# Turned groups' transfers to and from scratch issued by GpSimd in place of SyncE

## The chip, the cores and the metric

The kernel runs on one core of one Trainium2 chip. The metric is device time in microseconds: the median of 3 runs before the change is 1476.31 us (1476.15 to 1476.97).

## What is computed

The reference is one layer of a decoder trunk on 256 tokens of width 2048, in float32: a mixer (a state-space part with 32 heads and a gated short convolution), attention to 256 memory tokens, and a SwiGLU feed-forward part of width 5632. Each is added to the residual, with an RMS norm ahead of it, and a final norm follows. Cut to what matters:

```python
h = x
h = h + hybrid_mixer(rmsnorm(h, norm_mix), w_in, ..., w_out)     # 2048 -> 11296 -> 4096 -> 2048
h = h + memory_cross_attention(rmsnorm(h, norm_xa), rmsnorm(mem, mem_norm), w_q, w_k, w_v, w_o)
h = h + (silu(n @ w_gate) * (n @ w_up)) @ w_down                 # n = rmsnorm(h, norm_ffn)
return rmsnorm(h, norm_final)
```

Nearly all the work is products of 256 tokens with weights that are read once each.

## The kernel before

**Weights.** They come as a stream of 537 pieces, mostly 128 x 1024 (512 KB), in the order of a plan. SyncE loads each into one of 6 raw buffers, tile r (`load_to`, L214). ScalarE rounds it to a float32r high part, tile h (L254), and VectorE subtracts that from the piece to get the low part, tile l (L255); both have 4 buffers. TensorE then multiplies high by high, low by high and high by low: 12 matmuls of 512 columns for a piece, L328, L329 and L332. Some pieces are joined in pairs, where 7 products of blocks take the place of 8 (L657, L658, L660). For these, VectorE and ScalarE first form sums of the two pieces (`pair_sums`, L229 to L237), and corrections after it.

**Order.** The order of TensorE and SyncE is that of the code, since the kernel fixes it for those two engines. The instructions of ScalarE, VectorE and GpSimd are placed by a scheduler. The main loop runs in units of one or two pieces. `unit` loads some pieces ahead, calls the matmuls, and advances each of a list of generators by one step, so that work that follows a group of columns is spread over the next units.

**Turned groups.** A group of 512 columns is ready in PSUM with tokens on the partitions, and what follows needs features on the partitions. So VectorE transposes its 32 x 32 blocks (`turn_blocks`, L347, into tile b). `put` (L362) writes them to a scratch tile w in HBM with one DMA (L365), and `get` (L368) reads them back with one DMA (L372) in an order that moves the blocks to their places, 8 x 128 runs of 512 bytes, into tile f. There are 42 such groups:

- in the mixer, `group_post` (22 groups): what reads tile f there is L740, L848, L872 or L889
- after the output projection and after the attention, `to_features` (7 groups): L994 and L995
- in the attention, `heads` for keys and queries (2 groups): L1146 and L1148
- in the feed-forward part, `u_post` (11 groups): L1319 on ScalarE, then L1320 on VectorE

In the code there is one step of the generators, and so a unit, between the put, the get and the use; in `heads`, and in three calls of `to_features`, other numbers of steps. Both DMAs are issued by SyncE, in the place in its order where the generator calls them. Each waits there for what it needs: the put for VectorE's transposes, the get for the put's landing.

**GpSimd** has little to do: the masks of the decays (L714, L718), 24 in four runs of 6, each mask behind a load of decays that ScalarE's queue issues, and the small powers of the norms (L308, L903, L1400).

**The end of a group's work.** The norm's factor (L308) goes back to TensorE, which broadcasts it by transposes (`bcast`, L315), two units after it was asked for. The memory for DMAs that GpSimd issues is set when the program is built (`dynamic_dma_scratch_size=1024`, L1626); the change leaves that as it is.

Of the kernel before, what the change touches and what calls it, by code (L numbers as in the profile page):

```python
# [150 lines left out]
def trunk(tc, wst, vecs, xp, xtp, mp, mtp, wdt_in, nfin, outp):  # L151
    nc = tc.nc
# [8 lines left out]
    with ExitStack() as ctx:  # L161
# [18 lines left out]
        def nm(s):  # L180
            cnt[0] += 1
            return f"{s}{cnt[0]}"

        def slot(shape=(128, 512), dt=F32):
            return sp.tile(list(shape), dt, tag="s", name=nm("s"))
# [157 lines left out]
        def turn_blocks(src):  # L343

            t = bp.tile([128, 1024], F32, tag="b", name=nm("b"))
            for tb in range(2):
                nc.vector.transpose(t[:, tb * 512:tb * 512 + 512], src[tb])  # L347
            return t

        def scaled(accs, r, adds=None):  # L350

            o = [slot() for _ in range(2)]
            for tb in range(2):
                src = accs[tb]
                if adds is not None:
                    c, op = adds[tb]
                    tt(o[tb], src, c, op)
                    src = o[tb]
                act(o[tb], src, AF.Identity, scale=r[:, tb:tb + 1])  # L359
            return o  # L360

        def put(t):  # L362

            w = drp.tile([2, 128, 512], F32, tag="w", name=nm("w"), bufs=2)
            nc.sync.dma_start(w.rearrange("t p k -> p t k"), t.rearrange("p (t k) -> p t k", t=2))  # L365
            return w

        def get(w):  # L368


            d = fp.tile([128, 1024], F32, tag="f", name=nm("f"))
            nc.sync.dma_start(d.rearrange("p (x c) -> p x c", x=8),  # L372
                              w.rearrange("t (a i) (b c) -> (i b) (t a) c", a=4, b=4))
            return d.rearrange("p (x f j) -> p f x j", x=8, f=4)


# [218 lines left out]
        def group_post(n, accs):  # L595
            t = turn_blocks(scaled(accs, scales["x"], in_corr.pop(n, None)))
            yield
            w = put(t)
            yield
            d = get(w)  # L600
            yield
            if isinstance(groups[n], tuple):
                yield from posts[groups[n][0]](groups[n][1], d)
                return
            for f, (kind, _, j) in enumerate(groups[n]):
                p = posts[kind](j, d[:, f])
                if next(p, 0) is None:
                    procs.append(p)
                if f < 3 and not (kind == "xs" and j % 2 == 0):
                    yield  # L610
# [75 lines left out]
        for kt in range(KT):  # L686
            first_unit(kt)
            if kt == 10:
                c = 0
# [258 lines left out]
        for parts in in_units():  # L948
# [10 lines left out]
            _, n, c = keys[-1]  # L959
# [38 lines left out]
        def wait(k):  # L998
            for _ in range(k):
                yield  # L1000

        def to_features(n, gain, dst, steps=(1, 1, 1)):

            if steps is None:
                for i in range(2):
                    ps = msc()
                    for f in (2 * i, 2 * i + 1):
                        for tb in range(2):  # L1010
                            nc.tensor.transpose(ps[:, (f % 2) * T + tb * 128:(f % 2) * T + tb * 128 + 128],
                                                res[tb][n][:, f * 128:f * 128 + 128], ident)
                    for f in (2 * i, 2 * i + 1):
                        dst[4 * n + f] = gained(ps[:, (f % 2) * T:(f % 2) * T + T], gain, 4 * n + f)
                return
            t = turn_blocks([res[tb][n] for tb in range(2)])
            yield from wait(steps[0])
            w = put(t)
            yield from wait(steps[1])
            d = get(w)  # L1020
            yield from wait(steps[2])
            for f in range(4):
                dst[4 * n + f] = gained(d[:, f], gain, 4 * n + f)
# [86 lines left out]
        for i, parts in enumerate(units_o):  # L1110
            for j in (i, i + 1, i + 2):
                if j < len(units_o) and len(units_o[j][0]) == 2 and units_o[j][0][0] not in seven_a:
                    c = units_o[j][0][0][2]
# [6 lines left out]
            _, n, c = keys[0]  # L1120
# [12 lines left out]
        def heads(accs, r, dst, steps=(1, 1, 1)):  # L1133

            t = turn_blocks(scaled(accs, r))
            yield from wait(steps[0])
            w = put(t)
            yield from wait(steps[1])
            d = get(w)
            yield from wait(steps[2])  # L1140
            with tc.high_priority():
                for i in range(2):
                    a = slot()
                    o = a.rearrange("p (f x j) -> p f x j", f=2, x=8)
                    if i:
                        nc.vector.tensor_copy(o, d[:, 2:4])  # L1146
                    else:
                        nc.scalar.copy(o, d[:, 0:2])  # L1148
                    dst.append(a)

        KTs, Vs, qs = [], [], []
        for m, tiles in (("k", mh), ("q", h1g)):
            accs = [acc(), acc()]
            last = KT // 2 - 2
            for c in range(0, last, 2):
                unit([([(m, k)], lambda k=k: tok_mm(accs, (m, k), side_blocks(tiles, 2 * k), (0, 1), k == 0, False))
                      for k in (c, c + 1)])

            def last_mm(tb):
                for k in (last, last + 1):  # L1160
                    tok_mm(accs, (m, k), side_blocks(tiles, 2 * k), (tb,), False, k == last + 1)

            keys = [(m, last), (m, last + 1)]
            unit([(keys, lambda: last_mm(0)), (keys, lambda: last_mm(1))],
                 heads(accs, scales["mem"], KTs) if m == "k" else heads(accs, xa["sc"], qs, (2, 1, 0)))
# [96 lines left out]
        with tc.high_priority():  # L1262
            for mb in range(2):
                Vs.append(slot())
                c = scales["mem"][:, mb:mb + 1]
# [71 lines left out]
        for i, parts in enumerate(ffn_units()):  # L1337
# [6 lines left out]
            for part in parts:  # L1344
                m, n, c = part[0]
# [134 lines left out]
        for i, parts in enumerate(units):  # L1480
# [7 lines left out]
            if len(parts[0]) == 2:  # L1488
                _, n, c = keys[0]
# [141 lines left out]
```

## Time and profile before

| | |
|---|---|
| median of 3 runs | 1476.31 us |
| the profiled execution | 1478.79 us |
| its span | 1477.1 us |
| granted TensorE clock | 0.999 |
| busy: TensorE, VectorE, ScalarE, GpSimd | 99%, 87%, 60%, 3% |
| bytes from HBM and to it | 323.4 MB, 26.3 MB |

The span is the time from the first to the last instruction of one profiled execution. In the profile PE is TensorE, DVE VectorE, ACT ScalarE, POOL GpSimd and SP SyncE; SPq is SyncE's queue. A tile is named without its buffer's number. TensorE's matmuls overlap, so that a row of 390 ns stands for one every 227 ns. A wait is put down to what came last by the profile, and a wait of an engine that isn't the bound costs nothing by itself.

### The profile page before, as it was taken

The numbers are of one execution on the slowest core, as the hardware profiler recorded it, in microseconds if no ns is written. First come the engines' busy times: TensorE is split into PE (matmuls) and PEld (weight loads), VectorE is DVE, ScalarE is ACT, GpSimd is POOL, SyncE is SP. The second block draws the span as 40 slices with busy tenths as digits, with TensorE's granted clock in tenths as the row PEclk, the third lists the DMA queues.
The fourth block names the chain that finished last, engine by engine and source line by source line (L and its number), as shares of the span: only waits on it lengthen the run. The fifth ranks groups of instructions, "written<-read, shape, count | busy, mean of one in ns | idle before, by whom it ended". The sixth has DMA issues, their size and how long they took to land.

```text
span 1477.1 us, 18980 instructions
## 1 busy us (share of the span) xinstructions
PE 1461.6 (99%) x6568; PEld 1203.6 (81%) x6568; DVE 1279.7 (87%) x1865; ACT 885.4 (60%) x1263; POOL 38.5 (3%) x46
## 2 busy tenths in 40 slices
PE   9999999999999999999999999999999999999997
PEld 7778888888887888888888888888888887888886
DVE  6678899989999775897578999999999998979995
ACT  7576665967765544665466665556655554655663
POOL 0012000101000000000000000000000000000000
PEclk9999999999999999999999999999999999999999
DMA  9777758769677575777648766656676667765553
GB/s 362 248 251 263 259 202 296 253 215 313 224 258 261 193 262 188 253 270 279 224 171 295 265 220 224 220 215 225 228 247 247 220 228 229 268 228 190 195 201 112
DMA packets 151520, 350.91 MB, mean 238 GB/s; under 512 B 11616, under 2 KB 63232, under 8 KB 151424
## 3 DMA queue, kind: packets, MB, share of 16 engines
q1 hardware_dynamic: 142368, 342.83, 66.1%
q10 hardware_dynamic: 9056, 6.87, 1.6%
q8 instruction: 51, 0.84, 0.2%
q14 instruction: 45, 0.37, 0.1%
HBM read 323.40 MB, written 26.26 MB: 237 GB/s over the span
## 4 chain that ended last, share of the span: by engine, by line
PE 67%; DVE 1%; issue 0%; ACT 0%; DVEq 0%; POOLq 0%; POOL 0%
PE a L328 17%; PE a L329 17%; PE a L332 17%; PE m L660 3%; PE m L657 3%; PE m L658 3%; PE a L658 2%; PE a L657 2%; PE a L660 2%; PE m L1207 0%; PE m L1176 0%; PE m L804 0%; PE m L1195 0%; DVE g L1309 0%; DVE f L1292 0%
## 5 line engine op out<-in xcount | busy, mean ns | idle before, releaser
L254 ACT CAST h<-r 128x1024 fp32r<-128x1024 f32 (+1 forms) x539 | 562.3, 1047 | 401.7 <-PE a L329 190.0
L255 DVE TENSOR_TENSOR l<-r,h 128x1024 fp32r<-128x1024 f32 (+1 forms) x539 | 649.5, 1216 | 120.3 <-ACT h L254 114.9
L328 PE MATMUL a<-h,s 128*128 128x512 f32 x1671 | 655.0, 392 | 1.1 <-ACT h L254 1.1
L329 PE MATMUL a<-h,s 128*128 128x512 f32 x1671 | 651.0, 390 | 0.0
L332 PE MATMUL a<-l,s 128*128 128x512 f32 x1671 | 450.0, 390 | 0.0
L328 PEld LDWEIGHTS a<-h,s 128*128 128x128 f32 x1671 | 313.9, 188 | 68.2 <-ACT h L254 2.2
L332 PEld LDWEIGHTS a<-l,s 128*128 128x128 f32 x1671 | 313.7, 188 | 65.6 <-DVE l L255 0.4
L329 PEld LDWEIGHTS a<-h,s 128*128 128x128 f32 x1671 | 314.1, 188 | 64.0
L236 ACT CAST s<-b 128x512 fp32r<-128x512 f32 x110 | 67.6, 618 | 71.3 <-DVE b L229 65.4
L237 DVE TENSOR_TENSOR s<-b,s 128x512 fp32r<-128x512 f32 x110 | 75.6, 687 | 0.8 <-ACT s L236 0.7
L347 DVE STREAM_TRANSPOSE b<-s 128x512 f32<-128x512 f32 x62 | 40.9, 691 | 7.2 <-ACT s L359 7.2
L229 DVE TENSOR_TENSOR b<-r,r 128x512 f32<-128x512 f32 x55 | 37.7, 686 | 10.3 <-DMA r<-in_w_dram 9.8
L230 DVE TENSOR_TENSOR r<-r 128x512 f32<-128x512 f32 x55 | 37.9, 689 | 0.8
L232 DVE TENSOR_TENSOR r<-b,r 128x512 f32<-128x512 f32 x55 | 37.7, 686 | 0.1
L237 DVE TENSOR_TENSOR s<-r,s 128x512 fp32r<-128x512 f32 x55 | 37.7, 685 | 0.0
L236 ACT CAST s<-r 128x512 fp32r<-128x512 f32 x55 | 33.9, 617 | 6.2 <-DVE r L232 5.1
L231 DVE TENSOR_TENSOR b<-b,r 128x512 f32<-128x512 f32 x55 | 37.7, 685 | 0.0
L745 DVE SCALAR_TENSOR_TENSOR t<-t,vec,t 128x255 f32<-128x255 f32 (+2 forms) x72 | 32.4, 479 | 2.8 <-ACT t L742 2.3
L657 PE MATMUL m<-s,t 128*128 128x512 f32 x76 | 29.6, 389 | 0.0
L660 PE MATMUL m<-s,t 128*128 128x512 f32 x76 | 29.6, 389 | 0.0
L658 PE MATMUL m<-s,t 128*128 128x512 f32 x76 | 29.6, 389 | 0.0
L660 PE MATMUL m<-l,s 128*128 128x512 f32 x72 | 28.1, 391 | 1.2 <-DVE l L255 1.2
(248 smaller groups left out, 1395.4 us busy)
## 6 DMA issues: line engine op xcount, KB each, us to landing
r<-in_w_dram SPq DMA_DIRECT2D x535, 512.0 KB, 4.8
w<-b SPq DMA_DIRECT2D x42, 512.0 KB, 3.3
f<-w SPq DMA_DIRECT2D x42, 512.0 KB, 4.8
s<-acsT ACTq DMA_DIRECT2D x24, 256.0 KB, 5.5
s<-in_xt_dram SPq DMA_DIRECT2D x16, 256.0 KB, 6.9
s<-in_mt_dram SPq DMA_DIRECT2D x8, 256.0 KB, 5.2
s<-in_m_dram SPq DMA_DIRECT2D x8, 256.0 KB, 5.8
parked<-s SPq DMA_DIRECT2D x8, 256.0 KB, 8.1
```

What stands on the lines that cost most here:

```text
L230: tt(u[:, a], u[:, a], u[:, b], ALU.add)
L236: nc.scalar.copy(h, x)
L237: tt(l, x, h.bitcast(F32), ALU.subtract)
L254: nc.scalar.copy(h[:, c], r[:, c])
L255: tt(l[:, c], r[:, c], h[:, c].bitcast(F32), ALU.subtract)
L328: mm(ps[tb], ah, h[:, w], start=first and i == ks[0], stop=False)
L329: mm(ps[tb], al, h[:, w], start=False, stop=False)
L332: mm(ps[tb], blocks(i, tb)[0], l[:, i * 512:i * 512 + 512], start=False, stop=stop and i == ks[-1])
L347: nc.vector.transpose(t[:, tb * 512:tb * 512 + 512], src[tb])
L657: mm(ps, ah, bh, start=any(ps is q for q in start), stop=False)
L658: mm(ps, al, bh, start=False, stop=False)
L660: mm(ps, ah, bl, start=False, stop=any(ps is q for q in stop))
```

## The change

`put` and `get` have a new argument, the engine that issues the DMA, and it is GpSimd unless told otherwise. Only `heads` names SyncE. On GpSimd the get is two DMAs of 512 runs each, one for each half of the tokens; on SyncE it stays one. So 40 puts and 40 gets leave SyncE, and 40 puts and 80 halves of gets are added to GpSimd.

```diff
-        def put(t):
+        def put(t, queue=nc.gpsimd):
 
             w = drp.tile([2, 128, 512], F32, tag="w", name=nm("w"), bufs=2)
-            nc.sync.dma_start(w.rearrange("t p k -> p t k"), t.rearrange("p (t k) -> p t k", t=2))
+            queue.dma_start(w.rearrange("t p k -> p t k"), t.rearrange("p (t k) -> p t k", t=2))
             return w
 
-        def get(w):
+        def get(w, queue=nc.gpsimd):
 
 
             d = fp.tile([128, 1024], F32, tag="f", name=nm("f"))
-            nc.sync.dma_start(d.rearrange("p (x c) -> p x c", x=8),
-                              w.rearrange("t (a i) (b c) -> (i b) (t a) c", a=4, b=4))
+            for t in range(2) if queue is nc.gpsimd else (slice(0, 2),):
+                t = slice(t, t + 1) if isinstance(t, int) else t
+                queue.dma_start(d[:, t.start * 512:t.stop * 512].rearrange("p (x c) -> p x c", c=128),
+                                w[t].rearrange("t (a i) (b c) -> (i b) (t a) c", a=4, b=4))
             return d.rearrange("p (x f j) -> p f x j", x=8, f=4)
...
             t = turn_blocks(scaled(accs, r))
             yield from wait(steps[0])
-            w = put(t)
+            w = put(t, nc.sync)
             yield from wait(steps[1])
-            d = get(w)
+            d = get(w, nc.sync)
```

TensorE's order is the same before and after. From the get on, lines of the changed kernel have numbers that are higher by two (L374 for L372, L716 for L714, L747 for L745).

SyncE's order, where the second and the third turned group were handled (w is scratch, b the transposed blocks, f the features, r a raw buffer for weights). Before:

```order
L214 DMA r_722<-in_w_dram 128x1024
L214 DMA r_724<-in_w_dram 128x1024
L365 DMA w_780<-b_699 128x2x512
L214 DMA r_802<-in_w_dram 128x1024
L214 DMA r_813<-in_w_dram 128x1024
L372 DMA f_827<-w_780 128x8x128
L365 DMA w_829<-b_808 128x2x512
L214 DMA r_851<-in_w_dram 128x1024
L214 DMA r_853<-in_w_dram 128x1024
L372 DMA f_871<-w_829 128x8x128
L214 DMA r_893<-in_w_dram 128x1024
L214 DMA r_895<-in_w_dram 128x1024
```

and the same place after:

```order
L214 DMA r_723<-in_w_dram 128x1024
L214 DMA r_725<-in_w_dram 128x1024
L214 DMA r_803<-in_w_dram 128x1024
L214 DMA r_814<-in_w_dram 128x1024
L214 DMA r_853<-in_w_dram 128x1024
L214 DMA r_855<-in_w_dram 128x1024
L214 DMA r_896<-in_w_dram 128x1024
L214 DMA r_898<-in_w_dram 128x1024
```

The weight loads now stand one behind the other.

GpSimd's order from its first norm power on. Before, the first run of masks:

```order
L308 TENSOR_TENSOR rr_516<-rv_514,half 128x2
L714 AFFINE_SELECT s_750<-s_750 128x2x128
L718 AFFINE_SELECT s_752<-s_752 128x512
L714 AFFINE_SELECT s_754<-s_754 128x2x128
L714 AFFINE_SELECT s_756<-s_756 128x2x128
L718 AFFINE_SELECT s_758<-s_758 128x512
L714 AFFINE_SELECT s_760<-s_760 128x2x128
```

and after:

```order
L374 DMA f_828<-w_781 128x4x128 x2
L716 AFFINE_SELECT s_751<-s_751 128x2x128
L720 AFFINE_SELECT s_753<-s_753 128x512
L716 AFFINE_SELECT s_755<-s_755 128x2x128
L716 AFFINE_SELECT s_757<-s_757 128x2x128
L720 AFFINE_SELECT s_759<-s_759 128x512
L716 AFFINE_SELECT s_761<-s_761 128x2x128
L365 DMA w_831<-b_809 128x2x512
L374 DMA f_873<-w_831 128x4x128 x2
```

The third group's put and its two half gets now stand behind the six masks. Each of the other three runs of masks also has a put right behind it.

VectorE's order where the first pair of pieces is summed (t are steps of a convolution that reads the third group, L745 before and L747 after; L229 to L232 are the pair's sums). Before:

```order
L255 TENSOR_TENSOR l_933<-r_853,h_932 128x1024
L745 SCALAR_TENSOR_TENSOR t_922<-t_920,vec,t_922 128x255
L745 SCALAR_TENSOR_TENSOR t_922<-t_920,vec,t_922 128x254
L745 SCALAR_TENSOR_TENSOR t_972<-t_970,vec,t_972 128x255
L745 SCALAR_TENSOR_TENSOR t_922<-t_920,vec,t_922 128x253
L745 SCALAR_TENSOR_TENSOR t_972<-t_970,vec,t_972 128x254
L255 TENSOR_TENSOR l_979<-r_893,h_978 128x1024
L745 SCALAR_TENSOR_TENSOR t_972<-t_970,vec,t_972 128x253
L229 TENSOR_TENSOR b_982<-r_893,r_895 128x512
L230 TENSOR_TENSOR r_895<-r_895 128x512
L231 TENSOR_TENSOR b_982<-b_982,r_895 128x512
```

and after:

```order
L229 TENSOR_TENSOR b_985<-r_896,r_898 128x512
L882 SCALAR_TENSOR_TENSOR s_869<-u_871,vec,s_869 128x255
L255 TENSOR_TENSOR l_932<-r_853,h_931 128x1024
L882 SCALAR_TENSOR_TENSOR s_869<-u_871,vec,s_869 128x254
L255 TENSOR_TENSOR l_936<-r_855,h_935 128x1024
L230 TENSOR_TENSOR r_898<-r_898 128x512
L255 TENSOR_TENSOR l_982<-r_896,h_981 128x1024
L747 SCALAR_TENSOR_TENSOR t_925<-t_923,vec,t_925 128x255
L231 TENSOR_TENSOR b_985<-b_985,r_898 128x512
L747 SCALAR_TENSOR_TENSOR t_925<-t_923,vec,t_925 128x254
```

The pair's sums have moved ahead of the steps that need the turned group. In the feed-forward part VectorE's order is the same but for the last two groups.

## The prediction

> **What bounds the kernel now.** I read the page's busy times first, then what TensorE waited for. The columns of the second view are: who waited, for whom, microseconds in total, how often, the longest.
>
> ```profile
> span 1477.1 us, 18980 instructions
> PE 1461.6 (99%) x6568; PEld 1203.6 (81%) x6568; DVE 1279.7 (87%) x1865; ACT 885.4 (60%) x1263; POOL 38.5 (3%) x46
> ```
> ```profile
> PE m L660 <- DVE l L255: 2.1, 2, 1.2
> PE m L468 <- POOL U L464: 1.8, 1, 1.8
> PE a L328 <- ACT h L254: 1.1, 1, 1.1
> PE m L657 <- ACT s L926: 1.1, 1, 1.1
> PE m L657 <- ACT h L254: 1.0, 1, 1.0
> ```
>
> TensorE has work for all but 15.5 us of the span, and its waits for other engines sum to 7.1 us. Two of the rows belong to the first microseconds, before any turned group exists (L468, 1.8 us, and L328, 1.1 us). So 2.1 + 1.1 + 1.0 = 4.2 us in mid-kernel is all that a better feed can give back. There is little to win and no such limit on what can be lost.
>
> Next I read what SyncE's queue waits for, since the moved transfers stand in it.
>
> ```profile
> SPq L214 <- DVE l L255: 694.8, 276, 9.0
> SPq L365 <- DVE b L347: 162.0, 28, 15.0
> SPq L372 <- DMA w<-b: 66.6, 39, 3.8
> ```
>
> Most of SyncE's waiting is a weight load (L214) waiting until VectorE has released a raw buffer: that is harmless, the load could not start anyway. The other two rows are different. SyncE works in order, so while it waits with a put (L365) for VectorE's transposes, or with a get (L372) for the put to land, the weight loads behind it wait too. The worst such place, in the timeline of SyncE (start, length, what), and what ScalarE, VectorE and TensorE did after it (in brackets the idle time before, and what ended it):
>
> ```profile
> 66.30 0.38 SPq L372 DMA_DIRECT2D f<-w  x1
> 81.83 0.38 SPq L365 DMA_DIRECT2D w<-b  x1
> 82.30 1.26 SPq L214 DMA_DIRECT2D r<-in_w_dram  x2
> 85.79 0.38 SPq L372 DMA_DIRECT2D f<-w  x1
> 86.26 2.33 SPq L214 DMA_DIRECT2D r<-in_w_dram  x4
> ```
> ```profile
> 89.23 1.05 ACT L254 CAST h<-r 128x1024 fp32r<-128x1024 f32 x1 [2.15 <-DMA r<-in_w_dram]
> ```
> ```profile
> 90.31 1.22 DVE L255 TENSOR_TENSOR l<-r,h 128x1024 fp32r<-128x1024 f32 x1 [3.23 <-ACT h L254]
> ```
> ```profile
> 100.17 0.50 PE L657 MATMUL m<-h,s 128*128 128x512 f32 x1 [0.96 <-ACT h L254]
> 102.60 0.50 PE L660 MATMUL m<-l,s 128*128 128x512 f32 x1 [1.23 <-DVE l L255]
> ```
>
> SyncE stood at one put from 66.7 to 81.8 us, 15 us. No weight came in that time, ScalarE lost 2.15 us and VectorE 3.23 us, and ten microseconds later TensorE lost 0.96 + 1.23 = 2.2 us.
>
> **The change, part by part.** *Weight loads.* 80 waits leave SyncE (40 groups, a put and a get each; the two of the heads stay). The 2.2 us at 100 us should go: the loads come 10 us and more before they are used, and VectorE's order even takes the pair sums (L229 to L232) earlier there. What is late next at this place is the turned group itself, below. The wait for L926 (1.1 us, at 465 us) also follows a late weight:
>
> ```profile
> 452.60 1.06 ACT L254 CAST h<-r 128x1024 fp32r<-128x1024 f32 x1 [1.65 <-DMA r<-in_w_dram]
> ```
>
> VectorE is busy without a gap from there to the stall, so 1.65 us of earlier work could remove it; I count half, 0.6 us, as its order also moves. The other wait of the L660 row, 2.1 - 1.2 = 0.9 us at 1245 us, follows a burst of VectorE whose rows are the same after the change: nothing. Gain: 2.2 + 0.6 = 2.8 us.
>
> *SyncE's own issue time.* 80 x 0.38 us leave SyncE. It waits 694.8 us for VectorE's releases: nothing is gained by that.
>
> *The turned group on GpSimd.* Now a put and a get take 3.3 + 4.8 = 8.1 us from issue to landing:
>
> ```profile
> w<-b SPq DMA_DIRECT2D x42, 512.0 KB, 3.3
> f<-w SPq DMA_DIRECT2D x42, 512.0 KB, 4.8
> ```
>
> and, over all of them, in the view of tile w (both kinds) and in that of tile f (the get alone):
>
> ```profile
> DMA to landing us min/median/max: 2.8/4.2/8.7
> ```
> ```profile
> DMA to landing us min/median/max: 4.0/4.8/7.8
> ```
>
> No row shows a transfer issued by GpSimd. Call x what the chain grows by. Low end: both at their shortest, 2.8 + 4.0 - 8.1 = -1.3 us (a gain, if the transfers no longer queue behind weights). High end: both at their longest, 8.7 + 7.8 - 8.1 = +8.4 us. Between them I take an estimate from the engine's own speed on 128 partitions, two passes of the same form:
>
> ```profile
> 128.96 0.63 POOL L718 TENSOR_SCALAR_AFFINE_SELECT s<-s 128x512 f32<-128x512 f32 x1
> 131.29 1.61 POOL L718 TENSOR_SCALAR_AFFINE_SELECT s<-s 128x512 f32<-128x512 f32 x1
> ```
>
> Three issues of 0.63 to 1.61 us in place of two of 0.38 us make x = 1.1 to 4.1; I take the middle, 2.6. [...]
>
> What x costs in the feed-forward stage: the put, the get and the first use of one group, and VectorE over eight such groups (columns of the last: span, TensorE, weight loads, VectorE, ScalarE, GpSimd):
>
> ```profile
> 909.61 0.38 SPq L365 DMA_DIRECT2D w<-b  x1
> 912.64 0.38 SPq L372 DMA_DIRECT2D f<-w  x1
> ```
> ```profile
> 918.35 0.61 ACT L1319 CAST s<-f 128x512 fp32r<-128x512 f32 x1
> ```
> ```profile
> L1319 ACT CAST s<-f x22: 608/614/620, 832.7 to 1257.9; 128x512 fp32r<-128x512 f32 x22
> ```
> ```profile
> 867.00:1199.00 332.00, 332.00 (x1466) 275.01 (x1466) 318.71 (x409) 193.77 (x240) 0.00 (x0) 1.00 0.64 228
> ```
>
> The get lands at 912.6 + 4.0 to 4.8, 0.9 to 1.7 us before its use; I take 1.3. ScalarE and VectorE work in order, and the use stands as far behind the transposes as before (five of the L255 steps in VectorE's order). So they stand still for x - 1.3 us per group. VectorE has (332 - 318.7) / 8 = 1.66 us of idle time per group to make up for it. TensorE is untouched up to x = 3.0, and from there loses x - 3.0 in each of the 22 / 2 = 11 groups. At x = 2.6: nothing. If that cover goes, 11 us for each microsecond.
>
> In the mixer GpSimd has masks to do (L714, L718). Each of the four runs now has a put behind it, and three of these puts were issued before their run's end. First or last masks of the three runs, and two of the puts:
>
> ```profile
> 85.32 0.58 POOL L714 TENSOR_SCALAR_AFFINE_SELECT s<-s 128x256 f32<-128x256 f32 x1
> 127.50 1.50 POOL L714 TENSOR_SCALAR_AFFINE_SELECT s<-s 128x256 f32<-128x256 f32 x1 [41.60 <-DMA s<-acsT]
> 132.86 1.39 POOL L714 TENSOR_SCALAR_AFFINE_SELECT s<-s 128x256 f32<-128x256 f32 x1
> 358.66 0.40 POOL L714 TENSOR_SCALAR_AFFINE_SELECT s<-s 128x256 f32<-128x256 f32 x1
> ```
> ```profile
> 129.99 0.38 SPq L365 DMA_DIRECT2D w<-b  x1
> 354.31 0.38 SPq L365 DMA_DIRECT2D w<-b  x1
> ```
>
> The puts of 81.83, 129.99 and 354.31 become those of 85.9, 134.2 and 359.1: 4.1, 4.3 and 4.8 us late, with x some 7 us. What covers that is the split weights standing ready:
>
> ```profile
> ACT h L254 <- PE a L329: 190.0, 144, 2.1
> ```
>
> ScalarE mostly waits for TensorE to release one of four h buffers, so it is up to three chunks ahead. A chunk is 12 matmuls at 332 / 1466 = 0.226 us, 2.7 us, so the cover is about 8 us against 7, and less where VectorE lags. I charge 0.6 us for each of the three places, 1.8 us (bounds: 0 and 7 us each).
>
> Behind a get that waits on GpSimd stand the next put and the small powers of the norms (L308, L903). Their result is broadcast by TensorE (L315) two units later, 2 x 24 matmuls or 10.9 us, and that transpose is in no row of TensorE's waits now: no cost.
>
> Sum: -2.2 - 0.6 + 0 + 1.8 = -1.0 us. The profiled execution took 1478.79 us, 1.7 around its span and 2.5 over the median of 1476.31, so it would become 1477.8 and the median 1475.3. That is inside 0.2% (3 us), about what a measurement of this kernel can tell from no change.
>
> **The rivals.** *All the waits go and the groups come in time* (x near 0, masks covered): 4.2 us less, 1472.1. For it: the releases now hold no load. Against it: the burst at 1245 us keeps its order. Chance 0.24.
>
> *The late group makes VectorE the bound* in the feed-forward stage: at x = 4.1 the loss is 11 x 1.1 = 12.1 us, so 1475.3 + 12.1 = 1487.4. It decides from x = 3.0 on. For it: the margin of 0.9 to 1.7 us, and 96% busy VectorE. Against it: idle time of one engine may overlap the other's stall. At the high end, x = 8.4, it would be 59 us, 1534.3. Chance 0.26.
>
> *VectorE holds GpSimd up.* The same mask took 0.63 and 1.61 us, so something slows GpSimd by a microsecond at a time. If each of the three issues waits out one subtraction of 1.22 us (L255), x = 2.6 + 3.7 = 6.3, and 11 x 3.3 = 36 us: 1511.6. Chance 0.05. [...]
>
> *It does nothing of use:* loads wait for VectorE's releases whoever issues the groups, and groups are covered. 1476.3, chance 0.05. [...]
>
> **How the numbers follow.** My forecast has 0.40, between about 1473.4 and 1479.3. Within 0.2%: 0.40 + 0.05 = 0.45; faster 0.24; slower 0.26 + 0.05 = 0.31. The range starts at 1471.5, just past the case of all waits gone. It ends at 1490, which is x = 4.3; the port case (0.05), the far part of the late groups (some 0.08) and a little at the fast end stay out.
>
> **What would show it.** Right: TensorE's waits at 98 to 103 us are gone, ScalarE's total for late weights (DMA r) falls, and ScalarE's and VectorE's waits for f rise to 1 to 2 us per feed-forward group, without a wait of TensorE there. Put to first use shows x. Wrong: gaps of TensorE in each feed-forward group behind L255 (x over 3.0), gaps near 139 and 365 us of several microseconds (masks not covered), or a wait of TensorE at L315.

## The result and the profile after

The changed kernel takes 1656.28 us (median of 4 runs, 1646.93 to 1661.7) against 1476.64 us beside it: a ratio of 1.121, 95% interval 1.117 to 1.125. It is 180 us slower, where 1475.3 us and a range to 1490 us were forecast. The profiled execution took 1661.7 us. First its page: the span, the busy times, the granted clock by slices, and the chain that ended last.

```profile
span 1660.0 us, 19123 instructions
PE 1521.4 (92%) x6568; PEld 1220.3 (74%) x6568; DVE 1278.2 (77%) x1865; ACT 872.3 (53%) x1263; POOL 129.6 (8%) x166
PEclk9889899989998999999999899999999999999999
PE 34%; issue 18%; DVE 16%; DMA 11%; ACT 3%; POOL 2%; ACTq 0%; DVEq 0%; POOLq 0%
L255 DVE TENSOR_TENSOR l<-r,h 128x1024 fp32r<-128x1024 f32 (+1 forms) x539 | 648.5, 1217 | 123.0 <-ACT h L254 120.6
```

TensorE was busy for 99% of the span and is now at 92%. It carries a third of the chain, and its clock has dropped in six of the 40 slices, where none had dropped before. VectorE's subtraction still takes 1217 ns a piece, so VectorE did not get slower. What TensorE waits for:

```profile
PE a L332 <- DVE l L255: 42.7, 15, 7.8
PE m L662 <- DVE l L255: 32.6, 21, 6.5
PE a L328 <- ACT h L254: 16.9, 6, 6.0
PE a L328 <- ACT s L996: 8.2, 2, 7.8
```

The first three are split weights (h and l), the fourth is features (s), and ScalarE and VectorE make them. So the next view is what those two wait for; here are ScalarE's rows for the features f read back, and its row for late weights:

```profile
ACT s L1321 <- DMA f<-w: 66.3, 11, 10.0
ACT s L996 <- DMA f<-w: 50.1, 6, 12.5
ACT t L742 <- DMA f<-w: 43.6, 6, 8.9
ACT s L850 <- DMA f<-w: 31.2, 4, 8.7
ACT h L254 <- DMA r<-in_w_dram: 3.1, 7, 0.8
```

All four first rows are first uses of a turned group (L1319, L994, L740 and L848 of the kernel before). In the kernel before, L1319 had no such wait, and the rows of the other three and of the late weights were:

```profile
ACT h L254 <- DMA r<-in_w_dram: 21.9, 15, 3.6
ACT s L994 <- DMA f<-w: 5.6, 2, 3.9
ACT t L740 <- DMA f<-w: 4.3, 4, 2.0
ACT s L848 <- DMA f<-w: 2.7, 2, 1.8
```

VectorE's two others after the change:

```profile
DVE s L891 <- DMA f<-w: 33.1, 4, 12.2
DVE u L874 <- DMA f<-w: 19.6, 2, 13.2
```

And SyncE, free of all groups but the two of the heads, now waits above all for raw buffers:

```profile
SPq L214 <- DVE l L255: 1204.5, 403, 15.0
```

So the weights are hardly late for ScalarE any more (3.1 us), and the groups are. In the feed-forward stage, one group on GpSimd and then ScalarE at its first use:

```profile
960.83 0.71 POOL L365 DMA_DIRECT2D w<-b  x1 [26.35 <-DVE b L347]
965.50 0.79 POOL L374 DMA_DIRECT2D f<-w  x1 [3.96 <-DMA w<-b]
969.07 0.75 POOL L374 DMA_DIRECT2D f<-w  x1 [2.78 <-issue]
```
```profile
967.45 1.05 ACT L254 CAST h<-r 128x1024 fp32r<-128x1024 f32 x1
976.17 0.62 ACT L1321 CAST s<-f 128x512 fp32r<-128x512 f32 x1 [7.66 <-DMA f<-w]
```

Three things are to be seen. The put took 4 us to land. The second half of the get was issued 3.57 us behind the first, though nothing in GpSimd's order stands between them and its wait is put down to "issue". ScalarE, whose next instruction was that first use, stood 7.66 us at it, and no weight was rounded in that time. The trace has the landing of each DMA: in all 40 groups that GpSimd moves, the second half was issued 0.30 to 0.34 us after the first half had landed. From the put's issue to the last landing it takes 14.35 us in the median of the 40 groups and 8.25 before, so x, the chain's growth, is 6.1 us.

TensorE does the same matmuls in the same order before and after, so their start times can be subtracted, one by one. That gives the loss by stage: 104.3 us in the mixer (22 groups), 31.0 us in the stages between, 45.1 us in the feed-forward stage (11 groups), 2.5 us after it; 182.9 us in all.

Not all of it is waiting. TensorE behind its longest wait of this kind (the four matmuls of L332 take 1.07 us elsewhere), and the windows around it, whose columns are the window, its length, then busy time and count of PE, PEld, DVE, ACT and POOL, the clock, the DMA share and GB/s:

```profile
620.79 0.39 PE L329 MATMUL a<-h,s 128*128 128x512 f32 x1
628.43 2.08 PE L332 MATMUL a<-l,s 128*128 128x512 f32 x4 [7.25 <-DVE l L255]
```
```profile
625.00:628.40 3.40, 0.00 (x0) 0.00 (x0) 2.46 (x4) 1.73 (x3) 0.00 (x0) 0.61 0.02 7
628.40:632.50 4.10, 4.07 (x16) 2.60 (x18) 4.10 (x8) 2.33 (x3) 0.00 (x0) 0.50 0.69 219
632.60:640.00 7.40, 7.40 (x37) 6.03 (x34) 7.37 (x18) 2.23 (x5) 1.76 (x1) 1.00 0.66 229
```

In the gap the granted clock falls to half, at 625.7 us by its record, 4.6 us after the last matmul, and it stays there for 4.1 us of work. It fell to half behind shorter gaps too: at 335.6 and 1025.1 us, where the longest gaps just before were 1.7 and 2.0 us.

Of the 512-column matmuls, 138 are followed by the next one after 380 to 460 ns in place of 227: some 27 us. Of these, 119 lie in the 15 stretches of this profile in which the record has the clock at half: 24 us. In 62 places the next start came over 0.5 us later than in the kernel before; these sum to 134 us. The rest of the 182.9 us is made of smaller delays.

### The profile page after: what moved, and what is told of

It reads as the page before. It is cut to its first block, busy times and chain, and to the rows that moved or that the text cites. A ratio compares the mean times of both kernels' runs of the same rounds, so it can differ in the third digit from the quotient of the medians.

```text
span 1660.0 us, 19123 instructions
## 1 busy us (share of the span) xinstructions
PE 1521.4 (92%) x6568; PEld 1220.3 (74%) x6568; DVE 1278.2 (77%) x1865; ACT 872.3 (53%) x1263; POOL 129.6 (8%) x166
## 4 chain that ended last, share of the span: by engine, by line
PE 34%; issue 18%; DVE 16%; DMA 11%; ACT 3%; POOL 2%; ACTq 0%; DVEq 0%; POOLq 0%
PE a L328 9%; PE a L329 9%; PE a L332 9%; DVE l L255 6%; DMA f<-w 5%; DMA w<-b 4%; DVE s L237 2%; POOL f L374 1%; ACT h L254 1%; PE m L662 1%; DMA r<-in_w_dram 1%; PE m L659 1%; PE m L660 1%; PE a L659 1%; DVE b L347 1%
## 5 line engine op out<-in xcount | busy, mean ns | idle before, releaser
L255 DVE TENSOR_TENSOR l<-r,h 128x1024 fp32r<-128x1024 f32 (+1 forms) x539 | 648.5, 1217 | 123.0 <-ACT h L254 120.6
L328 PE MATMUL a<-h,s 128*128 128x512 f32 x1671 | 665.6, 398 | 25.3 <-ACT h L254 16.9
L254 ACT CAST h<-r 128x1024 fp32r<-128x1024 f32 (+1 forms) x539 | 551.7, 1042 | 244.2 <-PE a L329 130.8
L329 PE MATMUL a<-h,s 128*128 128x512 f32 x1671 | 660.4, 395 | 0.4 <-DVE s L997 0.4
L332 PE MATMUL a<-l,s 128*128 128x512 f32 x1671 | 459.3, 395 | 42.8 <-DVE l L255 42.7
L332 PEld LDWEIGHTS a<-l,s 128*128 128x128 f32 x1671 | 317.6, 191 | 116.5 <-DVE l L255 50.1
L328 PEld LDWEIGHTS a<-h,s 128*128 128x128 f32 x1671 | 319.5, 191 | 98.7 <-ACT h L254 21.2
L329 PEld LDWEIGHTS a<-h,s 128*128 128x128 f32 x1671 | 319.7, 191 | 67.6 <-DVE s L997 1.4
L365 POOL DMA_DIRECT2D w<-b x40 | 29.2, 729 | 785.0 <-DVE b L347 714.1
L374 POOL DMA_DIRECT2D f<-w x80 | 61.3, 766 | 349.3 <-issue 180.2
L229 DVE TENSOR_TENSOR b<-r,r 128x512 f32<-128x512 f32 x55 | 38.3, 696 | 23.7 <-DMA r<-in_w_dram 21.7
L1322 DVE TENSOR_TENSOR s<-f,s 128x512 fp32r<-128x512 f32 x22 | 15.1, 688 | 51.7 <-ACT s L1321 51.7
L1321 ACT CAST s<-f 128x512 fp32r<-128x512 f32 x22 | 13.6, 617 | 66.3 <-DMA f<-w 66.3
L747 DVE SCALAR_TENSOR_TENSOR t<-t,vec,t 128x255 f32<-128x255 f32 (+2 forms) x72 | 32.0, 477 | 13.1 <-ACT t L744 12.8
L997 DVE SCALAR_TENSOR_TENSOR s<-f,vec,s 128x256 fp32r<-128x256 f32 x28 | 12.2, 480 | 37.1 <-ACT s L996 37.1
L662 PEld LDWEIGHTS m<-l,s 128*128 128x128 f32 x72 | 14.1, 196 | 35.7 <-DVE l L255 33.4
```

Of the source, the lines that this page charges most:

```text
L229: tt(f[:, a], g[:, a], u[:, a], ALU.add)
L254: nc.scalar.copy(h[:, c], r[:, c])
L255: tt(l[:, c], r[:, c], h[:, c].bitcast(F32), ALU.subtract)
L328: mm(ps[tb], ah, h[:, w], start=first and i == ks[0], stop=False)
L329: mm(ps[tb], al, h[:, w], start=False, stop=False)
L332: mm(ps[tb], blocks(i, tb)[0], l[:, i * 512:i * 512 + 512], start=False, stop=stop and i == ks[-1])
```

## The experiments

Theory when they began: the group's chain is longer by x = 6 us, above all because the halves follow each other; ScalarE and VectorE stand at the first use and TensorE runs out of split weights. Rivals: GpSimd itself is slow or held up; the scheduler's new order on ScalarE and VectorE costs the time; cutting the get in two costs by itself.

**A larger scratch size, then one whole get.** The program's `dynamic_dma_scratch_size` is raised from 1024 to 1536, the rest stays, and every engine's order with it:

```diff
-    nc = bacc.Bacc("TRN2", ..., dynamic_dma_scratch_size=1024)
+    nc = bacc.Bacc("TRN2", ..., dynamic_dma_scratch_size=1536)
```

> The changed kernel with 1536 in place of 1024 bytes for GpSimd's DMAs; every engine's order is that of the changed kernel. Theory (the second half of each get waits until the first has landed, because the memory does not hold both, and the chain of put and get is 6.1 us longer than before): the second half is now issued under 1.5 us behind the first, the chain falls from 14.35 us to 9.5-10.5, PE's waits at L332 and L328 mostly go, the granted clock is back at 0.99, and the time is 1480-1505 us. Rival 1 (the two halves wait for another reason, GpSimd's own pace or the program): the second half still follows the first's landing by 0.33 us and the time stays at 1640-1660. Rival 2 (the scheduler's new order on VectorE and ScalarE costs it): the halves overlap but the time stays above 1600.

1550.8 us, ratio 1.051 (1.048 to 1.053). The same stage as above, one group on GpSimd:

```profile
939.31 0.72 POOL L365 DMA_DIRECT2D w<-b  x1 [39.32 <-DVE b L347]
944.01 1.52 POOL L374 DMA_DIRECT2D f<-w  x2 [3.98 <-ACT s L236]
```

The halves are issued back to back (0.76 us apart), the median chain falls to 11.4 us, and 105 us come back, the largest part. Only the size was changed, so the second half's wait came of the 1024. That two halves do not fit into it is the theory's reading; what a half takes of it no run here shows. The 74 us that are left are more than the theory had and less than Rival 2 had.

Then, with that size, the get as one DMA:

```diff
-            for t in range(2) if queue is nc.gpsimd else (slice(0, 2),):
+            for t in (slice(0, 2),):
```

> As the run with 1536 bytes, and each get is one DMA on GpSimd instead of two halves. Theory (only the length of the chain counts): chain 9-10.5 us, time 1478-1505 us, within 10 us of the run with two halves. Rival (that there are two halves costs by itself, in issue time on GpSimd): at least 15 us faster than with two halves at the same memory. Rival 2 (the order): above 1600.

1544.4 us, ratio 1.044 (1.042 to 1.047): 6.4 us for the cut, and again over what the theory had.

**The cut alone, on SyncE.** In the kernel before, each of the 40 gets is two halves, both issued by SyncE:

```diff
-            nc.sync.dma_start(d..., w...)
+            for t in range(2):
+                nc.sync.dma_start(d[:, t * 512:t * 512 + 512]..., w[t:t + 1]...)
```

> The kernel before with each get in two halves, all on SyncE; nothing on GpSimd. Theory (GpSimd's memory makes the halves wait for each other): on SyncE the halves are issued back to back, the get takes 4.6-5.4 us, and the time is 1475-1480 us. Rival (two DMAs into one tile wait for each other wherever they are issued): the second half comes after the first's landing here too, the get takes about 9 us, and the time is over 1560.

1477.0 us, ratio 1.000 (0.999 to 1.001). SyncE's halves do not wait for each other: they are issued 0.41 to 0.45 us apart. The cut costs nothing there.

**One of the two transfers.** First the puts alone on GpSimd, then, with one DMA per get and the size at 1536, the gets alone:

```diff
-        def get(w, queue=nc.gpsimd):
+        def get(w, queue=nc.sync):
```

> Only the puts on GpSimd; the gets stay on SyncE as one DMA each. Theory: put 4.0 us instead of 3.3 and get 4.8, so the chain grows by 0.7-1.3 us; SyncE no longer stands for VectorE at the put, but waits longer for the landing ahead of the get; time 1475-1483 us. Rival (a DMA on GpSimd is late behind the masks and in its own queue): puts issued over 3 us late in groups other than those behind masks, time over 1500.

```diff
-        def put(t, queue=nc.gpsimd):
+        def put(t, queue=nc.sync):
```

> Puts on SyncE, gets on GpSimd as one DMA each, with 1536 bytes. Theory (with both on GpSimd the transfers share the DMA engines with weight loads that SyncE no longer holds back, 1.6 loads in flight at a put of the mixer against 0.4 before): here SyncE still stands until the transposes are done, so the puts take 3.3-3.8 us as before, only the get is 0.6 us late and shares with loads; chain 9-10 us; time 1480-1505 us. Rival (a transfer on GpSimd is slow by itself): the get takes 5.8 us or more as it did with both there, and the time is over 1515.

1493.1 us (ratio 1.010, 1.009 to 1.012) and 1527.3 us (1.034, 1.033 to 1.036). Both are over what the theory had. The first is under its rival's 1500 us, and the second meets its rival's numbers. The view of DMA issues, with KB each and the median from issue to landing: puts alone,

```profile
f<-w SPq DMA_DIRECT2D x42, 512.0 KB, 4.1
w<-b POOLq DMA_DIRECT2D x40, 512.0 KB, 3.2
```

gets alone,

```profile
w<-b SPq DMA_DIRECT2D x42, 512.0 KB, 3.3
f<-w POOLq DMA_DIRECT2D x40, 512.0 KB, 7.1
```

and both on GpSimd, one DMA per get:

```profile
w<-b POOLq DMA_DIRECT2D x40, 512.0 KB, 3.9
f<-w POOLq DMA_DIRECT2D x40, 512.0 KB, 5.8
```

The same get of 512 KB takes 4.1 us on SyncE, 5.8 or 7.1 on GpSimd. It is slowest where SyncE stood at the put and then let its weight loads go.

**SyncE made to stand again.** If free loads are what slows the transfers, SyncE's standing should help:

```diff
             queue.dma_start(w.rearrange("t p k -> p t k"), ...)
+            if queue is nc.gpsimd:
+                nc.sync.dma_start(held_b, t[0:1, 0:16])
...
+            if queue is nc.gpsimd:
+                nc.sync.dma_start(held_w, w[0, 0:1, 0:16])
```

> Puts and gets on GpSimd as one DMA each (1472 bytes, since two small tiles are needed), and SyncE issues a DMA of 64 bytes where each put and each get stood before, which waits for the same things: the transposes, and the landing of the put. It adds 80 small DMAs and restores only SyncE's standing. Theory (loads that SyncE no longer holds back slow the transfers): loads in flight at a mixer's put fall from 1.6 to about 0.5, the mixer's puts from a mean of 5.3 us to under 4.3, the chain from 11.5 to 9-10, and the time from 1544 to 1480-1505 us. Rival 1 (GpSimd's own slowness): puts stay over 5 us and the time is 1530-1550. Rival 2 (the placing of the first uses on VectorE and ScalarE): short chains, and still over 1520.

1638.0 us, ratio 1.110 (1.108 to 1.112): worse than without them by 94 us, and the theory as put there falls.

```profile
w<-b POOLq DMA_DIRECT2D x40, 512.0 KB, 5.7
f<-w POOLq DMA_DIRECT2D x40, 512.0 KB, 7.0
```

What SyncE waits for is what GpSimd waits for too. So the loads held back are let go at the moment at which GpSimd issues, and the transfers took longer still.

**Another queue, without GpSimd.** Puts and gets on ScalarE's queue, one DMA each:

```diff
-        def put(t, queue=nc.gpsimd):
+        def put(t, queue=nc.scalar):
-        def get(w, queue=nc.gpsimd):
+        def get(w, queue=nc.scalar):
```

> Puts and gets on ScalarE's queue, one DMA each; ScalarE stands at each until what it needs is there, so its time is not to be compared, only the transfers' lengths. Theory S (a transfer on another queue than the weight loads' takes turns with them in the DMA engines, on SyncE's queue it goes ahead of the loads behind it): with two loads or more in flight the puts take over 5 us and the gets over 6.5, as on GpSimd (6.3 and 7.5), without loads 3.0-3.6 and 4.5-5. Rival (GpSimd's way of making transfers is what is slow): puts under 4.2 and gets under 5.6 us whatever is in flight, as on SyncE (4.0 and 5.4).

```profile
w<-b ACTq DMA_DIRECT2D x40, 512.0 KB, 3.5
f<-w ACTq DMA_DIRECT2D x40, 512.0 KB, 5.6
```

Its one run took 1503.7 us. From the issues and landings of all DMAs in the first 600 us, which hold the mixer, the mean microseconds of a transfer by how many DMAs other than the groups' own were in flight during it on average (number of transfers in brackets):

```
                               put: under 1   2 or more    get: under 1   2 or more
SyncE (kernel before)             2.98 (1)    4.04  (5)       5.06 (1)    5.43 (19)
SyncE put, GpSimd get                  -      3.55 (17)       4.75 (1)    8.18 (18)
GpSimd, both                      3.61 (3)    6.32  (7)       4.86 (5)    7.52  (7)
ScalarE's queue, both             2.87 (5)    5.81  (5)       4.49 (2)    7.57  (5)
```

On SyncE's own queue others in flight matter less: a get takes 0.4 us longer beside them, a put 1.1, with one transfer alone to compare with. On another queue, GpSimd's or ScalarE's alike, a put takes 2.7 to 2.9 us longer beside them, a get 2.7 to 3.4. So this part is no property of GpSimd, and the rival of the gets alone falls too.

This table does not tell loads that were in flight already when the transfer was issued from loads that were issued behind it. The same traces do. Mean microseconds in the mixer, for puts by the weight loads in flight at their issue, and for gets with two in flight at their issue by whether more were issued within 2 us behind them:

```
                          put: 0 or 1 ahead     2 ahead    get, 2 ahead: none behind   1 or more behind
SyncE (kernel before)             3.45 (20)    5.14  (2)                  4.89 (3)        5.39 (19)
GpSimd, puts alone                3.21 (14)    5.60  (7)                     -               -
GpSimd, both                      3.88  (9)    6.28 (10)                  5.10 (4)        7.37  (7)
```

Two things go with a longer transfer here. Loads already in flight do so on either queue (puts of 3.45 against 5.14 us on SyncE, as far as two puts show it, and of 3.88 against 6.28 with both on GpSimd); SyncE's standing had kept them away from the puts (0.4 loads in flight at a put of the mixer, 1.6 with both on GpSimd). Loads issued right behind it do so on another queue (gets of 5.10 against 7.37 us), and hardly on the loads' own (4.89 against 5.39). These are lengths alone: that the queues take turns in the DMA engines, as theory S has it, is not shown. That SyncE's stand-ins made things worse fits this, since they let the loads go just then.

**The order of ScalarE and VectorE.** The change also moved 468 places of VectorE's order and 249 of ScalarE's, as the scheduler places them. A table of the order in the kernel before is imposed on both engines (`at` are an engine's instructions in the table's order):

```diff
         trunk(tc, *aps, out)
+        impose(nc, tc)
...
+        for a, b in zip(at, at[1:]):
+            tc.add_manual_dep(b, a.name, info, reason="order")
```

With both transfers on GpSimd, one DMA per get and the size at 1536:

> Both on GpSimd, one DMA per get, 1536 bytes (1544 us), and now ScalarE and VectorE in exactly the order that they have in the kernel before, imposed by a table; only GpSimd's and SyncE's orders are those of the change. Theory O (the scheduler, which had placed the first uses for a shorter chain, moved 468 places of VectorE's order and 249 of ScalarE's ahead of what the chip delivers): the mixer's cover is back, the chain stays at 11-12 us, and the time is 1480-1500 us. Theory L (the length of the chain alone, the mixer having no cover): 1530-1550 us.

With the change as it is:

> The changed kernel as it is (1024 bytes, two halves, 1656 us) with ScalarE and VectorE in the order of the kernel before. Theory O: the feed-forward part's 45 us stay (a chain 6.1 us longer against a cover of 3), and of the mixer's 104 us less than half stay: 1540-1590 us. Theory L: 1635-1660 us.

With the puts alone on GpSimd:

> Only the puts on GpSimd (1493 us), with ScalarE and VectorE in the order of the kernel before. Theory O: the chain of puts on GpSimd and gets on SyncE is no longer than before (3.2 + 4.1 us in the middle), so nothing is left of the 16 us: 1474-1479 us, and SyncE's stand of 15 us ahead of the third put is gone with TensorE's 2.2 us at 98 to 103 us. Theory L or another cause (SyncE's longer stand at the get): 1485-1495 us.

1517.7 us (ratio 1.029, 1.027 to 1.031), 1627.3 us (1.102, 1.100 to 1.104) and 1484.6 us (1.005, 1.004 to 1.007). The new order cost 27, 29 and 8 us: a real part, and neither theory's whole. The second and third time lie just under what theory L had. In the first of them ScalarE still stands at first uses:

```profile
ACT t L742 <- DMA f<-w: 21.0, 6, 6.5
ACT s L850 <- DMA f<-w: 13.2, 3, 5.8
ACT s L1321 <- DMA f<-w: 12.2, 10, 2.8
```

**More room for the chain.** One more unit between get and use in the mixer (both on GpSimd, one DMA per get, size 1536, the scheduler's own order):

```diff
             d = get(w)
             yield
+            yield
             if isinstance(groups[n], tuple):
```

> As with both on GpSimd, one DMA per get and 1536 bytes (1544 us), and one more unit between the get and the first use in the mixer's 22 groups. Theory (TensorE loses what the longer chain exceeds its cover by): 5.4 us more of cover is over the 3-4 us that the mixer's chain has grown by, so the 54 us lost in the mixer mostly go and the 14 us behind it stay: 1485-1505 us. Rival (the loss in the mixer comes from loads and order, not from the chain's length): over 1520.

1521.3 us, ratio 1.031 (1.029 to 1.033). That is the rival's time, but the traces show where. The mixer's loss falls from 53.9 to 31.5 us. In its first 250 us it stays, 30.0 us against 28.7; behind them it falls from 25.2 to 1.5. So there the room took the loss away, as the theory had it, and at the start it did not; why is open.

Then the first uses are placed later on the two engines alone. The order is taken from a kernel whose chains have one DMA more, and imposed; the extra DMA is not in these kernels:

```diff
+            x = drp.tile([2, 128, 512], F32, ...)
+            queue.dma_start(x, w)
+            w = x
```

This order was imposed on three kernels: both on GpSimd with one DMA per get and the size at 1536, the change as it is, and the kernel before:

> Both on GpSimd, one DMA per get, 1536 bytes, as in the run with the order of the kernel before (1518 us); ScalarE and VectorE now stand in the order that the scheduler makes when each chain has one more DMA in it (a copy of the scratch tile, which is in the kernel that the order is taken from and not in this one). Theory C (TensorE loses what ScalarE and VectorE stand at first uses that are placed ahead of what the chip delivers): their standing in the mixer falls from 66 us to under 25, and the time to 1478-1495 us. Theory D (the results are then late where TensorE's fixed order needs them, so the chain's length costs whatever the order): 1505 us or more.

> The changed kernel (1024 bytes, two halves in sequence, chain 14.3 us) with the same order for longer chains. Theory C: most of the 180 us can be placed away, 1490-1560 us. Theory D: above 1600 us, as with the order of the kernel before (1627).

> The kernel before, transfers on SyncE, with the order that the scheduler makes when one more DMA is in each chain on SyncE. Theory C: the 10 us that ScalarE and VectorE stand in the mixer go, TensorE's waits were 4.2 us in all: 1473-1477 us. Theory D: later results cost, over 1479 us.

1687.8 us (ratio 1.143, 1.141 to 1.144), 1701.3 us (1.151, 1.150 to 1.153) and, on SyncE, 1531.5 us (1.037, 1.035 to 1.038). With the puts alone on GpSimd SyncE's order gave 1534.0 us (1.039, 1.037 to 1.040):

> Only the puts on GpSimd, with the same order as the run beside it on SyncE. Theory C: from 1484.6 us (order of the kernel before) to 1473-1479 us, a candidate to be faster than the kernel before. Theory D: 1483 us or more.

Theory C falls. In the first of them neither engine stands at a first use in the mixer any more, and TensorE waits for the late sums and for what hangs on the late groups:

```profile
PE m L659 <- ACT s L236: 43.6, 14, 10.5
PE m L790 <- ACT s L748: 27.0, 8, 15.1
PE m L662 <- DVE s L237: 17.3, 10, 2.0
```

That order overshot by far (first uses 23 us behind the landing in the median). So the first uses were moved by about x alone, from the order of the kernel before: each goes behind what its engine did until 2.5 us, or 3.5 us, after the get's landing.

> Both on GpSimd, one DMA per get, 1536 bytes, with the order of the kernel before (1518 us), but each first use that stood within 2.5 us behind its get's landing there (2 us after the mixer, 1 us in the feed-forward part) is moved behind what ScalarE or VectorE did in those 2.5 us: 34 places of VectorE's order and 64 of ScalarE's. Theory C' (there is a best place for the first use, at the landing that the chip delivers; far behind it, as in the order for longer chains, results are late, ahead of it engines stand): standing in the mixer falls from 66 us to under 45, time 1495-1512 us. Theory D (the chain's length costs whatever the place): 1514-1522 us.

> The same with 3.5 us in the mixer, 3 us behind it and 1.5 us in the feed-forward part: 73 places of VectorE's order and 92 of ScalarE's. Theory C': standing in the mixer under 35 us, 1485-1508 us. Theory D: 1514 us or more.

1511.2 us (ratio 1.022, 1.020 to 1.024) and 1505.1 us (1.020, 1.017 to 1.022), where 1517.7 us was the start. Standing in the mixer fell from 66 to 44 and 40 us, where the second was to be under 35. But the three profiled executions took about the same time (spans 1510.6, 1511.4 and 1510.5 us), and in each TensorE lost 32 to 33 us in the mixer. Some of the time can be placed away; that most of it can is not shown.

**The gain by itself.** In the kernel before, only the put at which SyncE stood 15 us is placed one unit later:

```diff
             t = turn_blocks(scaled(accs, scales["x"], ...))
             yield
+            if n == 2:
+                yield
             w = put(t)
```

> The kernel before; only the put of the mixer's third group, at which SyncE stood 15 us, stands one unit later, and its get and use with it. Theory (the 2.2 us that TensorE lost at 98 to 103 us came of the weights that SyncE held there): they go, 1473.5-1475.5 us. Rival (other work is late there next): no difference, within 0.7 us of before.

1477.2 us, ratio 1.000 (0.9995 to 1.001). Two rows of TensorE's waits in this kernel:

```profile
PE m L662 <- DVE l L255: 0.9, 1, 0.9
PE a L659 <- ACT s L236: 0.6, 1, 0.6
```

The second row is all that is left at 98 to 103 us: 0.6 us of waiting, of 2.2. So SyncE's stand did cause most of it, but a gain of that size does not show in the time.

## Why the prediction was wrong, point by point

**Where the 180 us went.** Undone one after the other: the size of 1024, with which the halves follow each other, 105 us, the cut in two 6 us, the scheduler's new order 27 us. The 41 us that then stay go with transfers that meet more weight loads, and with gets issued 0.7 us later (chain of 11.4 us in the mixer against 8.95). How these 41 divide between the two, and how much of them another placing would save, stays open.

**Weight loads: right, and too small to matter.** The loads came in time for ScalarE (its waits for them fell from 21.9 to 3.1 us). Moving one put on SyncE gave 1.6 of the 2.2 us. In the changed kernel TensorE waits 2.1, 3.4 and 2.2 us for ScalarE at the same place instead, right after ScalarE stood 8.9 us at the first use of the third group. (Where the prediction has no weight coming from 66.7 to 81.8 us, two loads still landed, at 67.5 and 69.7; the next one landed at 89.1.)

**The size of x: the step that failed first.** It took x = 2.6 us from "three issues of 0.63 to 1.61 us in place of two of 0.38 us". The issues took 0.71 to 0.91 us each, within what was assumed. But the chain is not issues alone, and x was 6.1 us, inside the bounds of -1.3 to 8.4 that the step itself had. Mean microseconds of a chain, mixer and feed-forward stage:

```
                                   mixer: put  to get  get   chain     feed-forward: put  to get  get   chain
before                                    3.60  0.02   5.32   8.95                   3.15  0.30   4.54   7.99
both on GpSimd, one get, size 1536        5.27  0.73   6.24  12.24                   3.96  0.65   4.97   9.59
two halves, size 1536                     5.16  0.59   6.36  12.12                   4.08  0.67   5.01   9.76
as changed                                5.58  0.88   8.64  15.09                   3.91  0.68   9.60  14.19
```

The halves behind each other are 3.0 us of it in the mixer and 4.4 in the feed-forward stage. With one get, a put of the mixer is 1.67 us longer than before and a get 0.92; that this comes of the weight loads rests on the two tables of transfers above. And 0.65 to 0.73 us pass from a landing to the next issue. No term stood for any of these. In the changed kernel the shortest put on GpSimd took 3.15 us and the shortest half of a get 3.07, and the medians were 4.0 and 3.8.

**The feed-forward stage: right mechanism, cover too wide.** It said that TensorE is untouched up to x = 3.0 and then loses 11 us for each microsecond. By group, from five of the kernels (one get; two halves, both with the size at 1536; SyncE's stand-ins; the change with the order of before; the change):

```
x, us                 1.6    1.8    4.3    5.7    6.2
TensorE's loss, us    0.1    0.5    2.5    3.4    4.1
```

So it is free to about 2 us, and then costs nearly what was said. The 3.0 were two terms: 1.3 us between landing and use, and 1.66 us of VectorE's idle time. The second held: at x = 4.3, 5.7 and 6.2 ScalarE stood 4.2, 4.9 and 6.0 us a group at the first use, and TensorE lost 1.5 to 1.9 us less than that. The first was the wrong one: ScalarE stood for all but 0.1 to 0.7 us of x. Why so little of the 1.3 us was there is open. The prediction's own formula gives 11 x 3.2 = 35 us at x = 6.2, and 45 were lost. The rival of the late group was thus right for this stage, and its price at x = 6.1, 1475.3 + 34 = 1509, was beyond the range, which ended at x = 4.3.

**The mixer: the step that failed by most.** It charged 1.8 us for three puts behind masks, and nothing for the other 19 groups, since "the split weights standing ready" would cover about 8 us. The masks came out about as said: three puts were issued 5.3, 4.2 and 2.4 us after their transposes, against 4.1, 4.3 and 4.8. The cover did not. Mean chain of the 22 groups, what ScalarE and VectorE stood in all at their first uses, and what TensorE lost until the mixer's end:

```
                                          chain    standing    TensorE's loss, us
before                                     8.95       9.7        0
puts alone on GpSimd, order of before      8.66      19.9        7.0
puts alone on GpSimd                       8.69      27.8       13.2
ScalarE's queue                           10.43      34.1       21.4
both, one get, order of before            11.41      66.3       32.9
both, one get                             12.24      97.7       53.9
as changed                                15.09     127.5      104.3
```

TensorE lost a third to four fifths of what the two stood. In the kernel before, they already stood at 9 of the 22 first uses. The row on which the 8 us rested (ScalarE waits 190 us for TensorE) sums over the whole span: it shows that there is slack somewhere, not at a first use. The puts alone have a mean chain that is no longer than before, but single ones up to 17.2 us (11.3 before), and SyncE, waiting with its gets, held its loads until the put had landed: 246.5 us in all, 66.6 before.

**The clock: no term.** About 24 of the 183 us of the profiled execution are matmuls that start every 427 ns in the median in place of 227, in the 15 stretches at half clock behind gaps.

**The order: read, and not costed.** The prediction counted it as a help that VectorE takes the pair sums earlier; the new order of the two engines cost 27 to 29 us.

**The other rivals.** VectorE does not hold GpSimd up (the port case of the prediction's range): its subtraction (1216 and 1217 ns) and GpSimd's issues (0.71 to 0.91 us) are even, and ScalarE's queue shows the same lengthening of transfers. That the change does nothing of use falls. TensorE's wait at L315 is 0.2 us, as said.

## What to carry to other kernels

When a transfer moves to another engine, cost it as a chain: what must land before the next is issued, whether the new queue issues back to back what is issued together (here the second half came 0.30 to 0.34 us behind the first's landing with the size at 1024, and 0.77 us behind the first's issue with 1536), and what is in flight on the other queues then. An in-order queue that holds loads back also keeps them away from the transfer at its head: here 0.4 weight loads were in flight at a put on SyncE, and 1.6 at one on GpSimd. A cover is read at the instruction that waits, in the stage where it waits: a wait summed over the span is none.

## What the runs showed of the hardware

- With `dynamic_dma_scratch_size` at 1024, the second of two DMAs of 512 runs each on GpSimd was issued 0.30 to 0.34 us behind the first one's landing in all 40 groups; with 1536 it was issued 0.77 us behind the first's issue in the median.
- On a queue other than the weight loads', 512 KB took 2.7 to 3.4 us longer beside two loads or more; on the loads' own queue 0.4 us (get) to 1.1 us (put), with one transfer alone to compare with. Gets with two loads in flight at their issue took 5.4 us on the loads' own queue and 7.4 on GpSimd's when more loads were issued right behind them, and 4.9 and 5.1 when none were.
- TensorE's granted clock was at half for 3.4 to 13.7 us at a time behind gaps, in 15 stretches of the changed kernel's profile, two of them where the longest gaps just before were 1.7 and 2.0 us; its matmuls of 512 columns started every 427 ns there in the median, every 227 ns elsewhere; in the kernel before none stands between its first 6 us and its last 5.
- The order of ScalarE's and VectorE's instructions alone cost 55 us on SyncE, where the transfers had not changed: it was an order made for chains that are one DMA longer.
